# An expert layer's rows fetched by indirect DMA through a slot-to-token table, in place of one-hot products

## The chip, the core and the metric

The kernel runs on one core of a Trainium2 chip. The metric is the device time of one execution in microseconds (us), median over several runs. Engines are named as in the profile: PE (TensorE matmul), PEld (its weight loads), DVE (VectorE), ACT (ScalarE), POOL (GpSimd), SP (SyncE); SPq, ACTq and POOLq are the sequencers that issue their DMAs and branches.

## The reference

One layer over 512 tokens of width 1024. A token mixer (retention and mLSTM) makes up the first 1000 us and isn't touched but for its last rows. Then comes a mixture of 32 experts: each token picks one of four groups and two of its eight experts.

```
u2 = modulate(layer_norm(x), sh2, sc2)              # (512, 1024), float32
g  = top_1(softmax(u2 @ w_rg + b_rg))               # group
e1, e2 = top_2(softmax((u2 @ w_re + b_re)[g]))      # two experts of 8
y  = sum over the two: weight * ((silu(u2 @ w_e1[e]) * (u2 @ w_e3[e])) @ w_e2[e])
out = layer_norm(alpha * x + g2 * y) * ln2_g + ln2_b
```

Each expert has two matrices of 1024 x 512 and one of 512 x 1024 in float32, 2 MB each; all 32 together are 96 loads, 201 MB. The tokens of an expert are gathered into slots; 1024 assignments fall on 32 experts, unevenly.

## The kernel before

**Blocks.** An expert's tokens are worked on in blocks of 32 slots. The number of blocks is data: for experts 0 to 31 it is 1 1 1 1 1 1 1 1 1 2 2 1 1 2 1 1 2 2 1 1 2 1 1 1 5 3 2 1 3 2 1 1, 48 in all. The block count `nblk[e]` is loaded into a register of every engine one expert ahead; block 2 is inside `If(n >= 2)` (line 1576), block 3 inside `If(n > 2)` (line 1580), later ones inside further branches in `several` (lines 1493 to 1523).

**Loads.** `load(n)` (lines 925 to 941) issues the 96 weight loads on SP's queue (line 936), in order of expert. They go into a ring of 10 slots, RING = (2, 6, 2): two slots that are there early, six that come free after the mixer, two in the pool of the expert loop. Load n+10 is issued by SP after expert n/3 has used slot n. From load 10 on a load also waits until load n - 3 has landed (lines 937 to 939), so at most three are under way.

**Rows of an expert.** The normalised rows u2 are held in three bf16 parts whose sum is the float32 value: `u2[0..2]`, made per 128 tokens by `part_1` (line 1254: the first part by ScalarE, the remainder written back into `UP`) and `part_2` (line 1260). A one-hot matrix (`one_hot`, line 1169, VectorE: position of a token among its expert's slots equals slot number) times these parts gives the rows of the slots, transposed as the next product wants them. For experts 0 and 1 that is done ahead of the loop, 128 tokens at a time as they come ready: `gather_of` (line 1173, products at line 1177). For the others `gather(e, GN)` (line 1414, products at line 1424) does it inside the loop for a group of 64 slots of each of two (experts 2, 3) or four experts (4 to 7, 8 to 11, and so on), 96 products of up to 256 columns; it stands in experts 1, 3, 7, 11, 15, 19, 23 and 27, between that expert's hidden and output products. `slots_in` (line 1428, copies at 1432) copies the 64 slots of the next expert from PSUM.

**One block.** `hidden_q` (line 1459, 64 products at 1464, 32 slots wide) makes both hidden matrices in PSUM; `swiglu` (lines 1445 to 1447) combines them on ScalarE and VectorE; `turned` (line 1450) transposes the result twice on TensorE (line 1454) and copies it on ScalarE (line 1456); `output_q` (line 1469, 32 products at 1475) multiplies by the third matrix and VectorE scales the result (line 1477). Rows are stored to `y_d` in memory: the first two blocks from `yt` on ScalarE's queue (lines 1573 and 1579), the third and later ones from the two halves of `yq` by four DMAs on GpSimd's queue (line 1505).

**Third and later blocks.** `more(b, xT)` (line 1479) makes the rows of blocks 3 and 4 (then 5 and 6) at once by another one-hot (line 1482) and 96 products of 64 columns (line 1488), copied by ScalarE and VectorE (lines 1490, 1491).

**Order.** TensorE's order in the loop is as written (`manual_schedule(engines={EN.PE})`, lines 1557 to 1583), and so is SP's; the other engines' instructions are placed by the framework's scheduler. In one expert TensorE does:

```
t0 = hidden_q(xT, w, 0, gated("t0"))
if e + 1 in groups: xg = gather(start, GN)
output_q(t0, w[2], yt[:, 0:256])
with tc.If(n >= 2):
    output_q(hidden_q(xT, w, 1, gated("t1")), w[2], yt[:, 256:512])
    with tc.If(n > 2):
        several(e, w, n, xT, yq)
```

Behind expert 31 an indirect DMA on GpSimd (line 1605, 8 of them) fetches the two result rows of each token from `y_d` through `yrow`, and the weighted sum and last norm follow.

## Time and profile before

| | |
|---|---|
| median of 3 runs | 1661.74 us (1660.68 to 1661.85) |
| profiled execution, its own time | 1671.75 us |
| its span in the trace | 1669.7 us |
| mean granted TensorE clock | 0.922 |
| busy: PE, PEld | 1402.2 us (84%), 1101.1 us (66%) |
| busy: DVE, ACT, POOL | 783.6, 426.4, 185.1 us |
| HBM read, written | 307.37 MB, 33.57 MB |
| token mixer and routing | up to 1000.8 us |
| experts 0 to 3 | 1000.8 to 1058.6 us |
| experts 4 to 23 | 1058.6 to 1413.6 us |
| experts 24 to 31 | 1413.6 to 1629 us |
| sum and last norm | 1629 to 1669.7 us |

The boundaries of the experts are the starts of their first hidden products (line 1464). The profiled execution is one run with the hardware profiler on; all times of rows are its own. A granted clock of 1 is 2.4 GHz on TensorE, half of it the lower level; between them lies the mean of a stretch that has both. The DMA share is the mean busy share of 16 DMA engines.

### The profile page before, as it was taken

How to read it: one execution, taken by the hardware profiler on the slowest of the kernel's cores; microseconds unless marked ns; L12 is line 12 of the kernel's file. 1: busy time of each engine (PE TensorE's matmuls, PEld its weight loads, DVE VectorE, ACT ScalarE, POOL GpSimd, SP SyncE). 2: the span in 40 equal slices, each digit the busy share in tenths (PEclk: the TensorE clock that was granted, in tenths of full speed). 3: DMA queues.
4: the chain of work that ended last, by engine and by line, in shares of the span. 5: the costliest groups of instructions: out<-in, count | busy, mean ns of one | idle time of the engine just before them, and what ended most of it. 6: DMA issues, size and time to landing. Idle time of an engine off the chain costs nothing. (4 is left out here: it accounts for less than half of the span.)

```text
span 1669.7 us, 28900 instructions
## 1 busy us (share of the span) xinstructions
PE 1402.2 (84%) x11759; PEld 1101.1 (66%) x11759; DVE 783.6 (47%) x1893; ACT 426.4 (26%) x768; POOL 185.1 (11%) x113
## 2 busy tenths in 40 slices
PE   5999988999999999999999956666657677777774
PEld 3887977989798988989887744443434344445431
DVE  7757277485656565574777882211111111111115
ACT  3422244353444444443432220000000000000001
POOL 0101055143100000000023340000000000100003
PEclk9999999999999999999999968997889889888787
DMA  9414964244412131121656668989999989348444
GB/s 351 126 64 142 291 222 150 88 155 122 113 52 70 58 95 58 57 70 65 210 190 202 262 253 334 363 321 366 376 383 381 362 356 419 126 165 318 183 171 154
DMA packets 155844, 344.12 MB, mean 206 GB/s; under 512 B 18152, under 2 KB 110712, under 8 KB 147396
## 3 DMA queue, kind: packets, MB, share of 16 engines
q1 hardware_dynamic: 147544, 328.38, 54.7%
q10 hardware_dynamic: 6252, 7.73, 1.3%
q0 software_dynamic: 1792, 4.85, 0.8%
q8 instruction: 129, 2.11, 0.5%
q14 instruction: 127, 1.04, 0.2%
HBM read 307.37 MB, written 33.57 MB: 204 GB/s over the span
## 5 line engine op out<-in xcount | busy, mean ns | idle before, releaser
L1464 PE MATMUL ps_h<-w,xT 128*32 128x256 f32 x3072 | 220.2, 438 | 92.5 <-DVE xT L1432 34.4
L1464 PEld LDWEIGHTS ps_h<-w,xT 128*32 128x32 f32 x3072 | 121.4, 126 | 193.4 <-issue 132.2
L187 DVE TENSOR_TENSOR w_lo<-raw,w_hi 128x1024 fp32r<-128x1024 f32 x96 | 128.9, 1366 | 25.6 <-ACT w_hi L186 25.5
L1446 DVE SCALAR_TENSOR_TENSOR t<-t,ps_h 64x256 f32<-64x256 f32 x48 | 19.8, 412 | 256.8 <-ACT t L1445 256.8
L1475 PE MATMUL ps_y<-w,hT 128*32 128x256 f32 x1536 | 117.2, 457 | 19.8 <-ACT hT L1456 18.4
L1445 ACT ACTIVATE t<-ps_h 64x256 f32<-64x256 f32 x48 | 18.1, 377 | 427.9 <-PE ps_h L1464 386.1
L186 ACT ACTIVATE w_hi<-raw 128x1024 fp32r<-128x1024 f32 x96 | 96.1, 1050 | 58.8 <-PE ps_t L207 18.0
L550 POOL TENSOR_TENSOR macc<-macc,mw 128x1024 f32<-128x1024 f32 x32 | 82.2, 2570 | 101.2 <-ACT mw L549 51.5
L1475 PEld LDWEIGHTS ps_y<-w,hT 128*32 128x32 f32 x1536 | 52.0, 125 | 61.2 <-ACT hT L1456 25.4
L206 PE MATMUL ps_q<-u_lat,w_hi 128*128 128x512 f32 x192 | 78.8, 410 | 2.4 <-ACT u_lat L312 1.7
L1424 PE MATMUL xg<-sg,u 128*128 128x256 bf16 (+1 forms) x768 | 80.1, 266 | 0.0
L1477 DVE TENSOR_TENSOR yt<-ps_y,g2q 128x256 f32<-128x256 f32 x43 | 18.3, 425 | 129.4 <-PE ps_y L1475 119.4
L207 PE MATMUL ps_q<-u_lat,w_hi 128*128 128x512 f32 x192 | 77.9, 406 | 0.2 <-DVE u_lat L313 0.2
L208 PE MATMUL ps_q<-u_lat,w_lo 128*128 128x512 f32 x192 | 77.7, 405 | 0.0
L1424 PEld LDWEIGHTS <-u 128*128 128x128 bf16 x768 | 70.5, 98 | 10.7 <-issue 3.3
L1432 DVE COPY xT<-xg 128x128 f32<-128x128 f32 (+1 forms) x120 | 30.0, 295 | 96.9 <-PE xg L1424 62.6
L1505 POOL DMA_DIRECT2D y_d<-yq x20 | 10.2, 510 | 577.0 <-DVE yq L1477 455.6
L206 PE MATMUL ps_g<-w_hi,u_lat 128*128 128x256 f32 x256 | 72.6, 284 | 0.0
L208 PE MATMUL ps_g<-w_hi,u_lat 128*128 128x256 f32 x256 | 72.6, 283 | 0.0
L207 PE MATMUL ps_g<-w_lo,u_lat 128*128 128x256 f32 x256 | 72.5, 283 | 0.0
L207 PE MATMUL ps_v<-w_lo,u_lat 128*128 128x256 f32 x256 | 72.3, 282 | 0.0
L206 PE MATMUL ps_v<-w_hi,u_lat 128*128 128x256 f32 x256 | 72.3, 282 | 0.0
(394 smaller groups left out, 3450.7 us busy)
## 6 DMA issues: line engine op xcount, KB each, us to landing
w<-in_w_e_dram SPq DMA_DIRECT2D x96, 2048.0 KB
raw<-in_w_in_dram SPq DMA_DIRECT2D x40, 1024.0 KB
mw<-in_w_ada_dram SPq DMA_DIRECT2D x32, 512.0 KB
y_d<-plain SPq DMA_DIRECT2D x28, 512.0 KB
wada<-in_w_ada_dram SPq DMA_DIRECT2D x4, 2048.0 KB
y_d<-yt ACTq DMA_DIRECT2D x43, 128.0 KB
tanh_d<-tg SPq DMA_DIRECT2D x16, 256.0 KB
br_d<-rt SPq DMA_DIRECT2D x16, 256.0 KB
```

The costliest lines, as they stand in the source:

```text
L186: S.activation(h_, r_, AF.Copy)
L187: V.tensor_sub(l_, r_, f32(h_))
L206: PE.matmul(ps, lh, rh, start=first, stop=False)
L207: PE.matmul(ps, lh, rl, start=False, stop=False)
L208: PE.matmul(ps, ll, rh, start=False, stop=last)
L550: G.tensor_add(acc, acc, w)
L1424: PE.matmul(xg[j // step][:, j % step], u2[s_][:, i, j * P:(j + 1) * P], sg[:, i], start=(i == 0 and s_ == 0), stop=(i == 3 and s_ == 2))
L1432: V.tensor_copy(xT[:, j:j + step, :], xg[j // step][:, :, n, :])
L1446: V.scalar_tensor_tensor(t, t, 1.0, ps[0:64, 0:256], op0=OP.add, op1=OP.mult)
L1464: PE.matmul(ps[32 * a:32 * a + 32, 0:256], x[:, kt, 32 * b:32 * b + 32], w[a // 2][:, kt, 256 * (a % 2):256 * (a % 2) + 256], start=(kt == ...
L1475: PE.matmul(py[32 * a:32 * a + 32, 0:256], hT[:, kt % 2, 32 * (kt // 2):32 * (kt // 2) + 32], w2[:, kt, 256 * a:256 * a + 256], start=(kt ...
L1477: V.tensor_mul(yq, py[:, 0:256], g2q)
```

## The change

Rows of slots are no longer made by one-hot products inside the loop. `part_1` also stores the float32 rows to `u_d` in memory on ScalarE's queue (each token's 1024 values as four rows of 256), and writes the remainder into `xrs` in place of `UP`; `keep(3)`, which stores `xrs[3]`, comes earlier. After the routing, VectorE works out for each assignment the place of its slot; eight indirect DMAs on GpSimd scatter the token numbers into a table `inv_d` in memory (zeroed at the start), four DMAs load it back as `inv`, one copy per quarter of the partitions, and VectorE adds the quarter's number. `fetch(at, ...)` is an indirect DMA on GpSimd: it takes 128 rows of 1 KB from `u_d`, that is 32 slots x four quarters, to 128 partitions. `facing` turns them with two transposes on TensorE and one VectorE copy into the form that `hidden_q` wants.

Experts 0 to 3 are still made by one-hot products, now all four ahead of the loop (`gather_of` 256 columns wide, in four banks). For expert e >= 4 the first 32 rows are fetched into `xr` (two buffers): those of experts 4 and 5 ahead of the loop, those of e + 3 in expert e behind the facing of e + 1, which stands between the hidden and the output product of e. The second 32 rows are fetched inside `If(n >= 2)` into `xr1` (one buffer) and turned there. Third and later blocks copy their column of the table to `ix` on GpSimd, fetch into `xr2`, and turn; their stores are on GpSimd's queue as before. `yq` holds one block in place of two. The three parts of u2 live in a pool that is closed before the loop; the ring gets an eleventh slot in the loop's pool.

```diff
-RING = (2, 6, 2)
+RING = (2, 6, 3)
+NC = 112
...
+    u_d = dram.tile([4 * T, 256], F32, name="u_d")
+    inv_d = dram.tile([32 * NC, 1], I32, name="inv_d")
...
+        SP.dma_start(inv_d.rearrange("(s c) o -> s (c o)", c=NC), plain[0:32, 0:NC].bitcast(I32))
...
-    u2p = root.enter_context(tc.tile_pool(name="u2p", bufs=1))
-    u2 = [u2p.tile([P, 4, D], BF, name=f"u2{s}") for s in range(3)]
...
+    u2 = [bc.tile([P, 4, D], BF, name=f"u2{s}") for s in range(3)]
...
+    own = moec.tile([P, 5], F32, name="own")
+    SP.dma_start(own, I["small"][:, 640:645])
+    owni = moec.tile([P, 5], I32, name="owni")
+    V.tensor_copy(owni, own)
...
-                PE.matmul(xg[j // 4][:, j % 4], u2[s_][:, i, j * P:(j + 1) * P], sg,
-                          start=(i == 0 and s_ == 0 and j % 4 == 0), stop=(i == 3 and s_ == 2 and j % 4 == 3))
+                PE.matmul(xg[j // 2][:, j % 2], u2[s_][:, i, j * P:(j + 1) * P], sg,
+                          start=(i == 0 and s_ == 0 and j % 2 == 0), stop=(i == 3 and s_ == 2 and j % 2 == 1))
...
-        eng.tensor_sub(UP[i][:, c], UP[i][:, c], u2[0][:, i, c])
+        S.dma_start(u_d[4 * P * i:4 * P * i + 4 * P, :].rearrange("(p a) f -> p (a f)", a=4)[:, c], UP[i][:, c])
+        eng.tensor_sub(xrs[i][:, c], UP[i][:, c], u2[0][:, i, c])
 
     def part_2(i, eng, js=slice(0, NK)):
         c = slice(js.start * P, js.stop * P)
-        S.activation(u2[1][:, i, c], UP[i][:, c], AF.Copy)
-        eng.tensor_sub(u2[2][:, i, c], UP[i][:, c], u2[1][:, i, c])
+        S.activation(u2[1][:, i, c], xrs[i][:, c], AF.Copy)
+        eng.tensor_sub(u2[2][:, i, c], xrs[i][:, c], u2[1][:, i, c])
...
-        xg = xg_banks(2, 2)
+        xg = [gps.tile([P, 2, 4, 64], F32, tag=f"g{a}", name="xg") for a in range(4)]
         for b in range(2):
-            one_hot(sg0[:, b], b, 0, 2)
+            one_hot(sg0[:, b], b, 0, 4)
...
+        keep(3)
...
-    def gather(e, GN):
-
-        sg = m1p.tile([P, 4, 4, 64], BF, tag="sg", name="sg")[:, :, 0:GN]
-        for i in range(4):
-            one_hot(sg[:, i], i, e, GN)
-        xg = xg_banks(GN, 4 if GN == 4 else 2)
-        step = NK // len(xg)
-        for j in range(NK):
-            for i in range(4):
-                for s_ in range(3):
-                    PE.matmul(xg[j // step][:, j % step], u2[s_][:, i, j * P:(j + 1) * P], sg[:, i],
-                              start=(i == 0 and s_ == 0), stop=(i == 3 and s_ == 2))
-        return xg
...
+    def slots_of(b):
+        return mb.tile([P, 2, 4, 32], F32, tag=f"xT{b}", name="xT", bufs=1 if b else 2)
+
+    def slots_in(n, b):
+
+        xT = slots_of(b)
+        for a in range(4):
+            V.tensor_copy(xT[:, :, a, :], xg[a][:, :, n, 32 * b:32 * b + 32])
+        return xT
+
+    def fetch(at, tag, bufs):
+
+        xr = mr.tile([P, 256], F32, tag=tag, name="xr", bufs=bufs)
+        G.indirect_dma_start(out=xr, out_offset=None, in_=u_d, in_offset=bass.IndirectOffsetOnAxis(ap=at, axis=0),
+                             bounds_check=4 * T - 1, oob_is_err=False)
+        return xr
+
+    def facing(xr, b, pool, tag):
+
+        pt = pool.tile([P, 512], F32, tag=tag, name="ps_x")[:, 0:256].rearrange("p (c q) -> p c q", c=2)
+        for c in range(2):
+            PE.transpose(pt[:, c, :], xr[:, c * P:(c + 1) * P], ident)
+        xT = slots_of(b)
+        V.tensor_copy(xT.rearrange("p c a s -> p c (a s)"), pt)
...
-    def more(b, xT):
-
-        sb = m1p.tile([P, 4, 64], BF, tag="sb", name="osb")
-        V.tensor_tensor(sb, iota[:, 0:64].rearrange("p (o s) -> p o s", o=1).to_broadcast([P, 4, 64]),
-                        rme[:, :, b:b + 1].to_broadcast([P, 4, 64]), op=OP.is_equal)
-        ps = hps.tile([P, 512], F32, tag="ph", name="ps_or").rearrange("p (j s) -> p j s", j=NK)
-        for j in range(NK):
-            for i in range(4):
-                for s_ in range(3):
-                    PE.matmul(ps[:, j], u2[s_][:, i, j * P:(j + 1) * P], sb[:, i],
-                              start=(i == 0 and s_ == 0), stop=(i == 3 and s_ == 2))
-        S.copy(xT[:, 0:4], ps[:, 0:4])
-        V.tensor_copy(xT[:, 4:8], ps[:, 4:8])
-
-    def several(e, w, n, xT, yq):
-
-        for b in range(2):
-            V.tensor_scalar(rme[:, :, b:b + 1], rm[:, :, e:e + 1], -64.0 * (b + 1), None, op0=OP.add)
-
-        base = nc.values_load(orow[0:1, e:e + 1], min_val=64 * NE, max_val=64 * NE + 1024)
-
-        def some(b, row):
-
-            y = yq[:, b, :]
-            output_q(hidden_q(xT, w, b), w[2], y)
+    def several(e, w, n, yq):
+
+        base = nc.values_load(ocol[0:1, e:e + 1], min_val=2 * NE, max_val=2 * NE + 32)
+
+        def some(col):
+
+            ix = mr.tile([P, 1], I32, tag="ix", name="ix", bufs=2)
+            G.tensor_copy(ix, inv[:, bass.ds(col, 1)])
+            x = facing(fetch(ix, "xr2", 2), 2, tps, "tp")
+            output_q(hidden_q(x, w, gated("t")), w[2], yq)
             for a in range(4):
-                stored(G.dma_start(y_d[bass.ds(row, 32), 256 * a:256 * a + 256], y[32 * a:32 * a + 32, :]))
+                stored(G.dma_start(y_d[bass.ds(col * 32, 32), 256 * a:256 * a + 256], yq[32 * a:32 * a + 32, :]))
 
         tc.mark_branch_hint_location(f"more{e}d", smin(n >> 2, 1), engines={EN.PE})
-        more(0, xT)
-        some(0, base)
+        some(base)
         with tc.If(n > 3, label=f"more{e}d"):
-            some(1, base + 32)
+            some(base + 1)
             with tc.If(n > 4):
-                more(1, xT)
-                some(0, base + 64)
+                some(base + 2)
                 with tc.If(n > 5):
-                    some(1, base + 96)
+                    some(base + 3)
                     with tc.If(n > 6):
-                        V.tensor_scalar(rme, rme, -64.0, None, op0=OP.add)
-                        with tc.For_i(6, n, 2) as i:
-                            V.tensor_scalar(rme, rme, -64.0, None, op0=OP.add)
-                            more(0, xT)
-                            for b in range(2):
-                                some(b, base + i * 32 - 64 + 32 * b)
+                        with tc.For_i(6, n) as i:
...
+        rb8 = m1p.tile([P, 8], I32, name="rb8")
+        V.tensor_copy(rb8, r8)
+        V.tensor_scalar(rb8, rb8, 5, None, op0=OP.logical_shift_right)
+        V.tensor_scalar(sel[:, 0, :], sel[:, 0, :], 1.0 / 32, None, op0=OP.mult)
+        V.scalar_tensor_tensor(sel[:, 0, :], r8, float(NC), sel[:, 0, :], op0=OP.mult, op1=OP.add)
+        pos = m1p.tile([P, 8], I32, name="pos")
+        V.scalar_tensor_tensor(pos, rb8, 1.0 - 32 * NC, sel[:, 0, :], op0=OP.mult, op1=OP.add)
+    tok = []
+    for n in range(8):
+        q_ = G.indirect_dma_start(out=inv_d, out_offset=bass.IndirectOffsetOnAxis(ap=pos[:, n:n + 1], axis=0),
+                                  in_=owni[:, n // 2:n // 2 + 1], in_offset=None, bounds_check=32 * NC - 1, oob_is_err=False)
+        for o in tok:
+            tc.declare_no_dep(q_.ins, o.ins, reason="each assignment has its own slot")
+        tok.append(q_)
+    inv = m1p.tile([P, NC], I32, name="inv")
+    for a in range(4):
+        G.dma_start(inv[32 * a:32 * a + 32, :], inv_d.rearrange("(s c) o -> s (c o)", c=NC))
+    V.tensor_tensor(inv, inv, owni[:, 4:5].to_broadcast([P, NC]), op=OP.add)
+    xr = {e: fetch(inv[:, 2 * e:2 * e + 1], "xr", 2) for e in (4, 5)}
...
+            yq = mr.tile([P, 256], F32, tag="yq", name="yq", bufs=1)
             xT = xnext
             tc.mark_branch_hint_location(f"more{e}a", smin(n >> 1, 1), engines={EN.PE})
-            t0 = hidden_q(xT, w, 0, gated("t0"))
-            if e + 1 in groups:
-                start = e + 1
-                GN = groups[start]
-                xg = gather(start, GN)
+            t0 = hidden_q(xT, w, gated("t0"))
+            if e + 1 < 4:
+                xnext = slots_in(e + 1, 0)
+            elif e + 1 < NE:
+                xnext = facing(xr.pop(e + 1), 0, *((tps, "tp") if e == 3 else (gps, f"g{e % 4}")))
+                if e + 3 < NE:
+                    xr[e + 3] = fetch(inv[:, 2 * e + 6:2 * e + 7], "xr", 2)
             output_q(t0, w[2], yt[:, 0:256])
             stored(S.dma_start(y_d[e * 64:e * 64 + 32, :].rearrange("s (a f) -> a s f", a=4), yt[:, 0:256]))
-            if e + 1 < NE:
-                xnext = slots_in(xg, e + 1 - start, GN)
             with tc.If(n >= 2, label=f"more{e}a"):
                 tc.mark_branch_hint_location(f"more{e}c", smin(n // 3, 1), engines={EN.PE})
-                output_q(hidden_q(xT, w, 1, gated("t1")), w[2], yt[:, 256:512])
+                x1 = slots_in(e, 1) if e < 4 else facing(fetch(inv[:, 2 * e + 1:2 * e + 2], "xr1", 1), 1, tps, "tp")
+                output_q(hidden_q(x1, w, gated("t1")), w[2], yt[:, 256:512])
                 stored(S.dma_start(y_d[e * 64 + 32:e * 64 + 64, :].rearrange("s (a f) -> a s f", a=4), yt[:, 256:512]))
                 with tc.If(n > 2, label=f"more{e}c"):
-                    several(e, w, n, xT, yq)
+                    several(e, w, n, yq)
             for m in range(3):
                 load(3 * e + m + sum(RING))
```

## Rows read from the trace of the kernel before

**Rows 1.** The head of the page.

```profile
span 1669.7 us, 28900 instructions
```

**Rows 2.** Busy time by stretch; columns: stretch, length, five engines, clock, DMA share, GB/s.

```profile
core 0: us, PE busy (x) PEld busy (x) DVE busy (x) ACT busy (x) POOL busy (x), PEclk, DMA share, GB/s
997.00:1001.00 4.00, 2.88 (x28) 2.65 (x31) 3.12 (x24) 0.49 (x4) 0.00 (x0) 0.59 0.60 184
1058.00:1413.00 355.00, 244.17 (x3028) 146.46 (x3028) 58.55 (x178) 17.01 (x52) 0.00 (x0) 0.88 0.95 369
1413.00:1629.00 216.00, 160.71 (x2252) 95.05 (x2252) 34.21 (x104) 13.26 (x40) 10.19 (x20) 0.85 0.51 198
```

**Rows 3.** Waits of SP's queue, 1039 to 1302 us; columns: us, waits, us to landing.

```profile
SPq L936 <- DMA w<-in_w_e_dram: 231.8, 45, 7.9
```

**Rows 4.** The load line's issues, 1039 to 1302 us; least/mean/most ns, first and last.

```profile
L936 SPq DMA_DIRECT2D w<-in_w_e_dram x45: 327/331/379, 1039.2 to 1301.9; - x45
```

**Rows 5.** The load line's issues, 1394 to 1396 us.

```profile
L936 SPq DMA_DIRECT2D w<-in_w_e_dram x1: 332/332/332, 1395.5 to 1395.5; - x1
```

**Rows 6.** Busy time of line 1424 alone; columns: stretch, length, PE, PEld, clock, share, GB/s.

```profile
1058.00:1413.00 355.00, 53.27 (x480) 46.57 (x480) 0.88 0.95 369
```

**Rows 7.** Timeline of expert 24: start, length, engine, line; in brackets its wait.

```profile
1413.58 3.97 PE L1464 MATMUL ps_h<-w,xT 128*32 128x256 f32 x64 [1.25 <-DMA w<-in_w_e_dram]
...
1419.78 2.54 PE L1475 MATMUL ps_y<-w,hT 128*32 128x256 f32 x32 [0.43 <-ACT hT L1456]
...
1422.07 4.78 PE L1464 MATMUL ps_h<-w,xT 128*32 128x256 f32 x64
...
1429.01 1.93 PE L1475 MATMUL ps_y<-w,hT 128*32 128x256 f32 x32 [0.36 <-ACT hT L1456]
...
1435.45 3.66 PE L1464 MATMUL ps_h<-w,xT 128*32 128x256 f32 x64 [0.46 <-ACT xT L1490]
...
1441.27 3.53 PE L1475 MATMUL ps_y<-w,hT 128*32 128x256 f32 x32 [0.37 <-ACT hT L1456]
...
1444.55 3.79 PE L1464 MATMUL ps_h<-w,xT 128*32 128x256 f32 x64
1444.84 0.42 DVE L1477 TENSOR_TENSOR yq<-ps_y,g2q 128x256 f32<-128x256 f32 x1 [4.39 <-PE ps_y L1475]
1445.59 2.30 POOL L1505 DMA_DIRECT2D y_d<-yq  x4 [449.66 <-DVE yq L1477]
```

**Rows 8.** Timeline ahead of expert 0: the last early products.

```profile
998.12 2.72 PE L1177 MATMUL xg<-sg,u 128*128 128x128 bf16 x24 [1.22 <-DVE sg L1170]
```

**Rows 9.** Groups by line, 900 to 1670 us: busy, mean ns, idle before.

```profile
L1605 POOL DMA_INDIRECT ys<-y_d,yrow x8 | 8.0, 1002 | 53.2 <-PE ps_z L1613 51.0 <-issue 2.1
...
L1206 PE MATMUL ps_t<-small,xr 128*128 128x128 f32 x32 | 5.8, 338 | 5.2 <-DVE xr L1196 5.2
```

**Rows 10.** The DMA view: a queue (packets, MB, share); issues (count, KB, us to landing).

```profile
q10 hardware_dynamic: 6252, 7.73, 1.3%
...
y_d<-yt ACTq DMA_DIRECT2D x43, 128.0 KB
...
y_d<-yq POOLq DMA_DIRECT2D x20, 32.0 KB, 3.0
...
ys<-y_d,yrow POOLq DMA_INDIRECT x8, 5.7
```

**Rows 11.** Timeline of ScalarE and its queue, 1145 to 1162 us.

```profile
1145.20 1.05 ACTq L1573 DMA_DIRECT2D y_d<-yt  x1
...
1160.78 1.03 ACTq L1579 DMA_DIRECT2D y_d<-yt  x1
1162.02 0.38 ACT L1445 ACTIVATE t<-ps_h 64x256 f32<-64x256 f32 x1 [11.77 <-DMA y_d<-yt]
```

**Rows 12.** Busy time of line 1488 alone, in two stretches; columns as Rows 6.

```profile
1453.00:1460.00 7.00, 5.03 (x96) 4.99 (x96) 0.61 0.09 21
1490.00:1495.00 5.00, 2.96 (x96) 2.84 (x95) 1.00 0.01 3
```

**Rows 13.** ScalarE's branch and its store, 1187 to 1200 us.

```profile
L1576 ACTq COMPARE_BRANCH  x1: 45/45/45, 1192.1 to 1192.1; - x1
...
L1573 ACTq DMA_DIRECT2D y_d<-yt x1: 1052/1052/1052, 1195.3 to 1195.3; - x1
```

More of the change, by code (lines that the diff above doesn't have):

```diff
@@ L974, in build @@
     Eb = bc.tile([P, 4, NE], BF, name="Eb")
-    rm = moec.tile([P, 4, NE], F32, name="rm")
+    rm = bc.tile([P, 4, NE], F32, name="rm")
     wk = moec.tile([P, 4, 2], F32, name="wk")
@@ L980, in build @@
     obase = moec.tile([P, NE], F32, name="obase")
-    orow = moec.tile([P, NE], I32, name="orow")
+    ocol = moec.tile([P, NE], I32, name="ocol")
     eoff = moec.tile([P, NE], F32, name="eoff")
     SP.dma_start(eoff, I["small"][:, 320:352])
+    own = moec.tile([P, 5], F32, name="own")
+    SP.dma_start(own, I["small"][:, 640:645])
+    owni = moec.tile([P, 5], I32, name="owni")
+    V.tensor_copy(owni, own)
     def permuted(name, src):
@@ L1162, in affine_a @@
         eng.tensor_add(dst, dst, bias)
-    def xg_banks(GN, n):
-        ts = [gps.tile([P, NK // n, GN, 64], F32, tag=f"g{a}", name="xg") for a in range(n)]
-        return ts
     def one_hot(sg, i, e, GN):
@@ L1267, in build @@
     lt3 = p2.tile([P, 1, 36], F32, tag="lt1", name="lt1")
-    sg0 = bc.tile([P, 4, 2, 64], BF, name="sg0")
+    sg0 = bc.tile([P, 4, 4, 64], BF, name="sg0")
     with tc.manual_schedule(engines={EN.PE, EN.DVE, EN.Activation, EN.Pool}):
@@ L1410, in build @@
     g2q = m1p.tile([P, 256], F32, name="g2q")
-    rme = m1p.tile([P, 4, 2], F32, name="rme")
     scat = []
-    def gather(e, GN):
-        sg = m1p.tile([P, 4, 4, 64], BF, tag="sg", name="sg")[:, :, 0:GN]
-        for i in range(4):
-            one_hot(sg[:, i], i, e, GN)
-        xg = xg_banks(GN, 4 if GN == 4 else 2)
-        step = NK // len(xg)
-        for j in range(NK):
-            for i in range(4):
-                for s_ in range(3):
-                    PE.matmul(xg[j // step][:, j % step], u2[s_][:, i, j * P:(j + 1) * P], sg[:, i],
-                              start=(i == 0 and s_ == 0), stop=(i == 3 and s_ == 2))
-        return xg
-    def slots_in(xg, n, GN):
-        xT = mb.tile([P, NK, 64], F32, tag="xT", name="xT")
-        step = 4 if GN == 2 else 2
-        for j in range(0, NK, step):
-            V.tensor_copy(xT[:, j:j + step, :], xg[j // step][:, :, n, :])
+    def slots_of(b):
[16 more added lines that the diff above has]
+        V.tensor_copy(xT.rearrange("p c a s -> p c (a s)"), pt)
         return xT
@@ L1530, in build @@
         SP.dma_start(g2q[32 * b:32 * b + 32, :], mod_d[3, 256 * b:256 * b + 256].rearrange("(o d) -> o d", o=1).to_broadcast([32, 256]))
-    groups = {0: 2, 2: 2, **{e: 4 for e in range(4, NE, 4)}}
-    start, GN = 0, 2
     nb = nc.values_load(nblk[0:1, 0:1], min_val=0, max_val=16)
     with tc.manual_schedule(engines={EN.DVE}):
-        xnext = slots_in(xg, 0, 2)
+        xnext = slots_in(0, 0)
         ov = m1p.tile([P, NE], F32, tag="ov", name="ov")
```

18 lines of the change are left out of this document (9 added, 9 removed).

## The prediction

> **What bounds the kernel now.** I read the span first [rows 1], then the busy time of the stretches of the expert loop [rows 2]. From 1058 to 1413 us (experts 4 to 23) TensorE has work for 244 of 355 us and the DMA share is 0.95; from 1413 to 1629 (experts 24 to 31) TensorE is busy for 161 of 216 us and the share falls to 0.51. The second stretch is a chain of TensorE, ScalarE and VectorE, since the weights lie ready. For the first, the waits of the load queue are to be seen: between 1039 and 1302 us it waited for its own earlier loads in 45 of its waits, 232 of 263 us [rows 3]. Those 45 loads stand 262.7/44 = 5.97 us apart [rows 4], 17.9 us for an expert's three. So in that stretch the transfers and the chain are nearly tied: 20 experts need 358 us of loads, and the chain took 355.
>
> How much could the first stretch give if TensorE cost nothing? A load is issued only when the one three before it has landed. Load 76 (counted from 0, by the order of issue) goes out at 1395.5 us [rows 5], so load 73, the second matrix of expert 24, was there by then. Expert 24 began at 1413.6 us [rows 7]. The floor is thus 18 us earlier, no more.
>
> **What goes.** Five gathers of one-hot products lie in the first stretch, 53.3 us together, 10.7 each [rows 6]. Without one, the hidden product's end and the output product stand 1441.27 - 1439.11 = 2.2 us apart [rows 7]; a gather fills these, so each gives 8.5 us: 42.5 in the first stretch, 8.5 at expert 3, 8.5 at expert 27. The three to five `more` products of the second stretch lie between an output product's end at 1430.94 and the next hidden product at 1435.45, 4.5 us [rows 7].
>
> **What comes, ahead of the loop.** The early products now take 256 columns. The last 24 stand ahead of expert 0 and took 2.72 us for 128 columns [rows 8], at a granted clock of 0.59 from 997 to 1001 us [rows 2]: twice that at most, +2.7; I take 2.4, and +1.0 for wider one-hots and for the copy to memory of the last rows, which must land before their tile is overwritten (0 to 3). Five more DMA issues on ScalarE's queue and the eight scatters, four table loads and two fetches on GpSimd's cost nothing: ScalarE is idle most of that time, GpSimd had nothing to do until 1445.59 [rows 7], and expert 4's rows are wanted only some 40 us later. If that cover went (VectorE's one addition to the table ahead of expert 1's work), expert 1 would slip by some 10 us, under the loads. With the gather at expert 3 gone, expert 4 starts 3.4 - 8.5 = -5.1 us.
>
> **The eleventh slot** I cost at nothing: the loads are paced by one another [rows 3], and in the second stretch they are early. It would be worth one load, 6 us, where loads decide; against that, the slot of load 9 now lies on memory that the last early product still reads, so that load starts some 6 us later.
>
> **The first 32 rows of experts 4 to 31** are fetched two experts ahead, about 35 us (355/20 x 2). Their two transposes of 0.34 us [rows 9] fall into the 2.2 us between hidden and output product: nothing. Their traffic counts only at the floor: a packet of the store queue took 1.3% of 16 x 1669.7 us over 6252 packets = 56 ns [rows 10], so 128 packets on 16 engines 0.44 us; 28 fetches up to expert 24 make 12 us. Floor: 1395.5 - 2 + 12 = 1405, 8.6 earlier than now.
>
> **The second 32 rows** are the term that decides. Eleven experts need them (43 stores of `yt`, 32 of them first blocks): six in the first stretch, and 24, 25, 26, 28, 29. Today the second hidden product starts at 1422.07, as the first output product ends [rows 7], 4.5 us after the first hidden product's end at 1417.55. Now a fetch must come first, and GpSimd issues it behind the fetch for expert e+3, whose tile is free only after this expert's transposes. Count from the hidden product's end: transposes 0.75, issue of the earlier fetch 1.0 [rows 9] with two short waits 0.3, landing L, two transposes 0.7, a VectorE copy with its waits 0.7: 3.45 + L against 4.5. The delay is L - 1.05.
>
> L is not in this trace. From below: 3.0 us, the 32 KB stores that GpSimd issues into quiet queues (the last gather's 5.7 us is for eight of 512 KB) [rows 10]. From above: a 128 KB store in the same 1 KB packets, issued at 1145.20 between loads, let go of the next store and of ScalarE's queue only at 1160.8 [rows 11]: 15.5 us. I take the middle, 9.3: the fetch is issued some 8 us after the previous expert's end has set off three loads of 6 us each, so about half of these are still ahead of it. Delay 8.2 us each; 3 for expert 29, when one load is left.
>
> **The third and later blocks.** Block 3 is fetched right behind block 2: 4.5 us become 1.4, -3.1. Block 4 (expert 24) follows today at 1444.55 without a gap [rows 7]. Its fetch will stand behind the stores of block 3 in GpSimd's queue: VectorE's 0.42 at 1444.84, the stores from 1445.59 for 2.30 [rows 7], index copy and branch 0.5, landing 4.0 (quiet by then; 3.0 to 15.5), transposes and copy 1.4, minus what runs beside: +9.0. Block 5 pays the same less its old products (5.03 us [rows 12] and 1.4 around them): +2.6.
>
> **The clock.** An order product took 2.96 us where the clock was 1.00 and 5.03 at 0.61 [rows 12]. A hidden product behind a wait of 8 us starts at the low level. It takes 3.66 us at the high one [rows 7], 7.3 at worst; I take +1.2 for each of 13 blocks that wait (0 to 3.7).
>
> **Sum.** First stretch: -5.1 + 6 x 8.2 - 42.5 + 6 x 1.2 = +8.8, so expert 24 starts at 1422, past the floor of 1405: the chain decides. Second stretch: expert 24 8.2 - 3.1 + 9.0 + 2.6 = 16.7; 25 5.1; 26 8.2; 27 -8.5; 28 5.1; 29 3; clock 7 x 1.2 = 8.4: +38. Behind expert 31 nothing changes. Together +46.8 on the profiled execution's 1671.75 us, which is itself 10 us above the median of 1661.74; carried to the median, 1708.
>
> **Rivals.** *The fetch lands as in quiet queues* (L 3.5). For: GpSimd's own stores do [rows 10]. Against: the share of 0.95 [rows 2] and [rows 11]. Delays of 2.5 each; the first stretch then ends at the floor, -8.6; the second is 11 - 0.6 + 2.5 - 8.5 - 0.6 + 2.5 + 3 = +9: 1662, no change. By the Trainium skill ("DMA: Bandwidth & Descriptors", section "Anatomy of one DMA") a DMA from GpSimd costs 2.0 us and its bytes at 436 GB/s, an estimate of 2.3 us for 128 KB. The 15.5 us of [rows 11] speak against it in the first stretch; by it the sum would be some 1657.
>
> *The fetch of the second rows is issued early* (faster). If GpSimd's queue has the branch of expert e ahead of the fetch for e+3, it is a whole expert early, and a second block costs 1.4 us. First stretch at the floor, -8.6; second stretch 9.9 - 1.7 + 1.4 - 8.5 - 1.7 + 1.4 + 2 = +3: 1656. For it: ScalarE's store at 1195.3 stands behind the branch at 1192.1 though the program has it ahead [rows 13], so such an order occurs. Against: that store's input came late, while the fetch waits only for transposes ahead of the output product. It decides from the point where the fetch is issued over 10 us ahead of need.
>
> *The clock and the load queue cost more.* With every delayed block at the low level throughout, 3.7 + 1.9 us for 13 blocks, 73 in place of 16: 1765; with L at 15.5 and the clock as taken, 1771. For: both levels are in [rows 12]. Against: the mean stays at 0.85 in a stretch that waits a good deal already [rows 2]. The Trainium skill ("TensorE: Matmul & The Clock Gate", section "Part 1: The HAM clock gate") says that low is the resting state, and that only activity lifts it; a change that takes dense products away and adds waits would lose by it. The rows agree on the two levels.
>
> *The change does not do what it says*: the extra slot runs no load earlier because loads wait for loads. That is my forecast for it already.
>
> **Chances.** Forecast 0.42 (its own range 1680 to 1740), quiet fetch 0.22, early fetch 0.20, dearer 0.16. Some 0.2% is what a measurement of this kernel can tell from no change: 1658.4 to 1665.1. Of the quiet case 0.06 falls below, 0.10 inside; of the early one 0.17 below, 0.03 inside. Faster 0.23, same 0.13, slower 0.64. The range reaches to 1652, short of the early case's best, and up to 1760, into the dearer one.
>
> **What would show it.** Right: the DMA issues of `xr` from GpSimd, those of second blocks with 8 us and more to landing; TensorE's transposes of these rows waiting some 8 us for a DMA in eleven experts; expert 24 starting near 1422; block 4 waiting about 9 us for a fetch issued behind four stores. Wrong: a landing of 3 to 5 us between loads, or second fetches issued before their expert begins, with expert 24 at about 1405 and load waits ending the idle time of hidden products.

## The result: 1744.6 us after 1661.2, and where the 83 us lie

The changed kernel took 1744.64 us (median of 4 runs, 1742.04 to 1747.41), the kernel before 1661.21: a ratio of 1.0507, interval 1.0484 to 1.0530. The profiled executions differ by 1742.04 - 1671.75 = 70.3 us, their spans by 1740.4 - 1669.7 = 70.7; the rest is that the one shown of before lies 10 us above its median and the one of after 2.6 below. The head of the page after:

```profile
span 1740.4 us, 26902 instructions
```

Its busy time by stretch (experts 0 to 3, 4 to 23, 24 to 31; columns as in [rows 2]):

```profile
1001.30:1069.30 68.00, 30.06 (x395) 15.57 (x395) 11.46 (x48) 2.62 (x8) 13.21 (x15) 0.75 0.78 304
1069.30:1441.90 372.60, 215.77 (x2602) 108.22 (x2604) 41.95 (x104) 17.03 (x52) 26.00 (x26) 0.82 0.89 358
1441.90:1697.30 255.40, 152.82 (x1806) 74.91 (x1806) 30.41 (x78) 11.79 (x36) 26.90 (x40) 0.79 0.46 180
```

TensorE has 28 us less to do in experts 4 to 23 than in [rows 2] (215.8 for 244.2), and yet they take 372.6 us for 355: the DMA share fell from 0.95 to 0.89 and the granted clock from 0.88 to 0.82. Neither engine nor loads bound it; it waits. The stages, from the starts and ends of hidden and output products in both timelines:

| stage | before | after | forecast | measured |
|---|---|---|---|---|
| up to expert 0 | 1000.8 | 1001.3 | +3.4 | +0.5 |
| experts 0 to 3 | 57.8 | 68.0 | -8.5 | +10.2 |
| experts 4 to 23 | 355.0 | 372.6 | +13.9 | +17.6 |
| experts 24 to 31 | 215.1 | 255.4 | +38.0 | +40.3 |
| behind | 41.0 | 43.1 | 0 | +2.1 |
| sum | 1669.7 | 1740.4 | +46.8 | +70.7 |

**Expert 1 waits for the table.** The timeline between expert 0 and 1:

```profile
1016.88 0.97 POOL L1552 DMA_INDIRECT inv_d<-owni,pos  x1 [0.30 <-issue]
1023.45 2.05 POOL L1559 DMA_DIRECT2D inv<-inv_d  x4 [5.60 <-DMA inv_d<-owni,pos]
1033.41 0.28 DVE L1560 CUSTOM_DVE_ANT_0 inv<-owni,inv 128x224 uint16<-128x224 uint16 x1 [16.84 <-DMA inv<-inv_d]
1035.27 5.08 PE L1473 MATMUL ps_h<-w,xT 128*32 128x256 f32 x64 [24.43 <-DVEq L1581]
1035.36 0.62 DVE L1426 COPY xT<-xg 128x64 f32<-128x64 f32 x4 [1.68 <-DVEq L1581]
```

The last scatter is issued at 1016.9, the table's loads from 1023.4, and VectorE sits in front of its one addition for 16.8 us. Everything that VectorE and TensorE do for expert 1 is queued behind it: a gap of 24.4 us in place of 2.2.

**A second block waits for its rows.** Expert 9 in the timeline:

```profile
1155.20 0.44 PE L1440 MATMUL ps_x<-small,xr 128*128 128x128 f32 x2
1155.91 1.00 POOL L1432 DMA_INDIRECT xr<-u_d,inv  x1 [16.23 <-PE ps_x L1440]
1157.21 1.00 POOL L1432 DMA_INDIRECT xr<-u_d,inv  x1 [0.30 <-issue]
1157.77 3.54 PE L1484 MATMUL ps_y<-w,hT 128*32 128x256 f32 x32 [0.43 <-ACT hT L1465]
...
1165.66 0.66 PE L1440 MATMUL ps_x<-small,xr 128*128 128x128 f32 x2 [4.35 <-DMA xr<-u_d,inv]
...
1166.84 5.84 PE L1473 MATMUL ps_h<-w,xT 128*32 128x256 f32 x64 [0.52 <-DVE xT L1442]
```

The second fetch goes out 1.3 us behind the one for expert 12 and its rows are turned 8.4 us later. The second hidden product starts 11.6 us after the first ends (1155.20 to 1166.84); in [rows 7] it was 4.5. Over the six such experts of the stretch what follows the first output product grew from 50.0 to 98.0 us. The clock costs too: this product takes 5.84 us at a granted clock of 0.50 in its first us and 0.62 over its length; the same product took 3.66 us at 1.00 before.

**Later blocks and expert 29.** Expert 24's fourth block and the second block of 29, in the timeline:

```profile
1485.91 2.33 POOL L1499 DMA_DIRECT2D y_d<-yq  x4 [29.44 <-DVE yq L1486]
...
1488.75 1.09 POOL L1432 DMA_INDIRECT xr<-u_d,ix  x1 [0.32 <-POOL ix L1495]
1491.68 0.66 PE L1440 MATMUL ps_x<-small,xr 128*128 128x128 f32 x2 [6.54 <-DMA xr<-u_d,ix]
...
1647.13 0.44 PE L1440 MATMUL ps_x<-small,xr 128*128 128x128 f32 x2
...
1654.69 1.08 POOL L1432 DMA_INDIRECT xr<-u_d,inv  x1 [9.53 <-issue]
1659.67 0.66 PE L1440 MATMUL ps_x<-small,xr 128*128 128x128 f32 x2 [8.05 <-DMA xr<-u_d,inv]
```

Block 4's fetch stands behind the four stores of block 3 and then lands in 2.9 us, with no load under way. At expert 29 GpSimd comes 7 us late to its fetch. What held it is in its queue at line 1503, the end of the branch of expert 28 (waits, and their first and last start):

```profile
L1503 POOLq EVENT_SEMAPHORE  x5: 17/43/43, 1645.1 to 1651.1; - x5
...
L1503 POOLq INC_SWDGE_SEM  x1: 1657/1657/1657, 1651.2 to 1651.2; - x1
```

It leaves that branch only when its own four stores, issued from 1642.8, have landed, the last at 1650.9.

### The profile page after: what moved, and what is told of

It is laid out like the page before. It is cut to its first block, busy times and chain, and to the rows that moved or that the text cites. A ratio compares the mean times of both kernels' runs of the same rounds, so it can differ in the third digit from the quotient of the medians.

```text
span 1740.4 us, 26902 instructions
## 1 busy us (share of the span) xinstructions
PE 1353.7 (78%) x10695; PEld 1027.2 (59%) x10695; DVE 759.3 (44%) x1794; ACT 425.9 (24%) x764; POOL 237.0 (14%) x174
## 5 line engine op out<-in xcount | busy, mean ns | idle before, releaser
L1473 PE MATMUL ps_h<-w,xT 128*32 128x256 f32 x3072 | 235.2, 466 | 133.4 <-PEq L1567 66.5
L1454 ACT ACTIVATE t<-ps_h 64x256 f32<-64x256 f32 x48 | 18.1, 377 | 587.0 <-PE ps_h L1473 587.0
L1442 DVE COPY xT<-ps_x 128x256 f32<-128x256 f32 x44 | 18.7, 425 | 302.4 <-PE ps_x L1440 302.2
L1484 PE MATMUL ps_y<-w,hT 128*32 128x256 f32 x1536 | 124.8, 481 | 20.4 <-ACT hT L1465 17.5
L1432 POOL DMA_INDIRECT xr<-u_d,inv x39 | 39.4, 1010 | 458.9 <-PE ps_x L1440 420.5
L1440 PE MATMUL ps_x<-small,xr 128*128 128x128 f32 x88 | 22.5, 345 | 76.1 <-DMA xr<-u_d,inv 63.0
L906 POOL TENSOR_TENSOR raw<-raw,g 128x2048 f32<-128x2048 f32 x4 | 18.5, 4636 | 450.9 <-PE ps_b L214 417.1
L212 PE MATMUL ps_v<-w_hi,u_lat 128*128 128x256 f32 x256 | 72.2, 282 | 0.0
L214 PE MATMUL ps_v<-w_hi,u_lat 128*128 128x256 f32 x256 | 72.0, 281 | 0.0
```

What stands on the lines that cost most here:

```text
L212: PE.matmul(ps, lh, rh, start=first, stop=False)
L214: PE.matmul(ps, ll, rh, start=False, stop=last)
L906: G.tensor_mul(raw, raw, g1.rearrange("p (o f) -> p o f", o=1).to_broadcast([P, NK, 256]))
L1432: G.indirect_dma_start(out=xr, out_offset=None, in_=u_d, in_offset=bass.IndirectOffsetOnAxis(ap=at, axis=0), bounds_check=4 * T - 1, oob_i ...
L1440: PE.transpose(pt[:, c, :], xr[:, c * P:(c + 1) * P], ident)
L1442: V.tensor_copy(xT.rearrange("p c a s -> p c (a s)"), pt)
```

## The experiments

Every kernel is the changed one with the edit shown. The ratios are to the kernel before on the same chip; its median was 1657.5 to 1664.6 us there, so that medians of different rows are compared by their ratios where a few us matter. Stage lengths are worked out as in the table above; whole spans of single profiles are compared with care, since expert 0 started anywhere from 997.6 to 1007.1 us in kernels that don't differ ahead of it.

| kernel | median, us | ratio to before |
|---|---|---|
| changed kernel | 1744.64 | 1.0507 (1.0484 to 1.0530) |
| table_add_on_gpsimd | 1733.89 | 1.0453 (1.0404 to 1.0502) |
| second_rows_early | 1691.16 | 1.0211 (1.0159 to 1.0264) |
| two_loads_under_way | 1744.58 | 1.0505 (1.0444 to 1.0566) |
| one_load_under_way | 1866.81 | 1.1250 (1.1190 to 1.1309) |
| ten_slots | 1744.08 | 1.0468 (1.0404 to 1.0531) |
| later_stores_on_scalar | 1729.65 | 1.0399 (1.0342 to 1.0456) |
| second_rows_first | 1744.79 | 1.0483 (1.0425 to 1.0541) |
| second_rows_first_in_order | 1748.30 | 1.0501 (1.0461 to 1.0542) |
| early_rows_and_table | 1726.32 | 1.0376 (1.0333 to 1.0420) |
| rows_early_stores_on_gpsimd | 1661.17 | 1.0007 (0.9983 to 1.0032) |
| rows_early_gpsimd_in_order | 1686.94 | 1.0152 (1.0122 to 1.0182) |
| rows_early_add_on_vector | 1675.09 | 1.0080 (1.0052 to 1.0109) |

### The table's addition

```diff
-    V.tensor_tensor(inv, inv, owni[:, 4:5].to_broadcast([P, NC]), op=OP.add)
+    G.tensor_tensor(inv, inv, owni[:, 4:5].to_broadcast([P, NC]), op=OP.add)
```

> Only the addition to the table is moved from VectorE to GpSimd. Theory (the addition held VectorE, and with it the copies for expert 1, until the table had landed, and nothing covers that): the 24.4 us ahead of expert 1 become 2 to 4, expert 4 starts near 1048 instead of 1069.3, expert 24 near 1421 instead of 1442, and the median is about 1724. Rival (the wait was covered by the weight loads): the gap closes, but hidden products of experts 5 to 12 then wait for weights, expert 24 still starts near 1442, and the median stays within 5 us of 1744.

The gap fell to 7.3 us, but experts 0 to 3 take 59.2 us and not 47, and the median gained half of what was expected. The timeline shows the next in line:

```profile
1015.01 4.93 PE L1473 MATMUL ps_h<-w,xT 128*32 128x256 f32 x64 [7.29 <-DVEq L1581]
...
1030.67 0.37 POOL L1560 TENSOR_TENSOR inv<-inv,owni 128x112 int32<-128x112 int32 x1 [8.39 <-DMA inv<-inv_d]
...
1039.09 1.10 POOL L1432 DMA_INDIRECT xr<-u_d,inv  x1 [8.05 <-DMA y_d<-yt]
...
1047.54 0.41 PE L1440 MATMUL ps_x<-small,xr 128*128 128x128 f32 x2 [4.25 <-DMA xr<-u_d,inv]
```

Expert 4's rows are fetched 8 us after the addition, behind a branch in GpSimd's queue, and land 8.4 us later; expert 3's transposes wait for them. So the wait was on the path, as the theory says, and the rival falls: experts 5 to 12 don't wait for weights. But the table itself is late, and only part of the gap is to be had.

### How long a fetch takes to land

```diff
-            tc.add_manual_dep(loads[n].ins, loads[n - 3].ins.name,
+            tc.add_manual_dep(loads[n].ins, loads[n - 2].ins.name,
```

and the same with n - 1.

> A weight load waits for the one two before it instead of three. Theory (landing is long because of the loads that lie ahead in the DMA engines): second rows land about 6 to 7 us after their issue instead of 8.5, loads keep a pace of 6 to 6.5 us and stay ahead of the products, and the median is 15 to 28 us lower, near 1722. Rival (landing is set by GpSimd's queue and by the fetch ahead of it): landing stays at 8 to 9 us and the median within 5 us of 1744.

> A weight load waits for the one just before it. Theory: second rows land in about 5 us, as the one of expert 29 did with one load under way; the loads themselves now stand about 8 us apart, 24 us for an expert where the products take 18.6, so that experts 5 to 24 wait for weights and the median is some 1800. Rival (landing is set by GpSimd's queue): landing stays at 8 to 9 us. What tells them apart is the time from issue to transposes, not the median.

From the issue of the second rows to their transposes, in experts 9, 10, 13, 16, 17 and 20: 8.4, 9.3, 8.8, 8.2, 7.9, 8.1 us in the changed kernel (mean 8.4); 7.3, 8.1, 8.5, 7.6, 7.9, 7.8 with two loads (7.9); 5.4, 3.9, 3.3, 3.7, 3.0, 3.6 with one (3.8). Expert 10 in the timeline of the kernel with two loads:

```profile
1179.84 1.00 POOL L1432 DMA_INDIRECT xr<-u_d,inv  x1 [0.30 <-POOLq L1586]
...
1187.96 0.66 PE L1440 MATMUL ps_x<-small,xr 128*128 128x128 f32 x2 [5.64 <-DMA xr<-u_d,inv]
```

The same in the timeline of the kernel with one:

```profile
1217.26 1.00 POOL L1432 DMA_INDIRECT xr<-u_d,inv  x1 [0.30 <-issue]
...
1221.14 0.41 PE L1440 MATMUL ps_x<-small,xr 128*128 128x128 f32 x2 [1.41 <-DMA xr<-u_d,inv]
```

The busy time over experts 4 to 23, with two loads and with one (columns as in [rows 2]):

```profile
1070.70:1453.30 382.60, 228.54 (x2600) 112.33 (x2601) 41.95 (x104) 17.05 (x52) 25.98 (x26) 0.79 0.90 345
1073.30:1563.20 489.90, 237.97 (x2602) 112.33 (x2603) 41.94 (x104) 17.05 (x52) 26.00 (x26) 0.73 0.70 257
```

The same two fetches in the same order take some 8 us or, in five of six, under 4, so it isn't GpSimd's queue: that rival falls. In experts 9, 13, 16 and 20 of the kernel with one load the transposes waited for no DMA, so that their times are upper bounds. But the number of loads ahead isn't the measure either, as the first expectation had it: with two under way the DMA engines are as full (share 0.90 in this stretch), and landing and median stay; with one the share is 0.70, and the fetch lands in half the time, though a load was under way at each of the six. That it is the share that decides fits the three kernels and isn't shown beyond them. The price is the weights: 489.9 us for 60 loads, 8.2 each, and a median of 1867 where some 1800 was expected.

### Second rows fetched one expert early

```diff
+    xr1 = {}
...
                 if e + 3 < NE:
                     xr[e + 3] = fetch(inv[:, 2 * e + 6:2 * e + 7], "xr", 2)
+                xr1[e + 1] = fetch(inv[:, 2 * e + 3:2 * e + 4], "xr1", 2)
...
-                x1 = slots_in(e, 1) if e < 4 else facing(fetch(inv[:, 2 * e + 1:2 * e + 2], "xr1", 1), 1, tps, "tp")
+                x1 = slots_in(e, 1) if e < 4 else facing(xr1.pop(e), 1, tps, "tp")
...
+            xr1.pop(e, None)
```

> The second 32 rows of expert e + 1 are fetched in expert e, for every expert from 4 on whether it has a second block or not, into two buffers. Theory (the second block waits for a fetch that is issued just before it and lands 8.5 us later under weight loads): the transposes of second rows follow the first output product without a DMA wait, what follows the first output product in an expert of two blocks falls from about 16.5 us to 8 or 9, expert 24 starts at 1400 to 1412 (then the load pace of about 6 us each decides, slack 0 to 5 us), the last stretch is some 45 us shorter, and the median is about 1665 (1655 to 1685). Rival (GpSimd's queue, which takes its fetches one behind another, is the limit): 28 more fetches make first rows late too, and the median is 1744 or more.

The wait is gone in every expert: what follows the first output product fell from about 16.5 to about 10 us (98.0 to 60.6 over six), experts 4 to 23 from 372.6 to 346.4. The median gained 53 us (49 by the ratios) of the 80 expected. Part of the rest lies in the first hidden products of experts 4 to 23, which took 122.0 us for 108.2 in the changed kernel; what made them longer isn't shown. Expert 24 now waits for its weights, in the timeline:

```profile
1411.12 0.63 PE L1473 MATMUL ps_h<-w,xT 128*32 128x256 f32 x4 [2.74 <-DMA w<-in_w_e_dram]
...
1417.10 4.97 PE L1473 MATMUL ps_h<-w,xT 128*32 128x256 f32 x60 [5.35 <-DMA w<-in_w_e_dram]
```

These waits come to 8.1 us, no more than the gaps of 4.8 and 3.5 us ahead of and inside the same product in the changed kernel. But since expert 24 is early, the fetch of its fourth block, still behind the stores, meets loads under way: 10.2 us to land instead of 2.9.

### The eleventh slot

```diff
-RING = (2, 6, 3)
+RING = (2, 6, 2)
```

> RING is (2, 6, 2) again. Theory (in the changed kernel weights lie ready 16 us and more before their hidden product, so a slot more or less moves no product): the smallest margin falls by some 6 us to about 10, the median stays within 5 us of 1744. Rival (the extra slot is what kept experts 5 to 24 fed): hidden products wait for weights and the median rises by 10 us or more.

As the theory had it: 1744.08 for 1744.64. The smallest margin is expert 9's: by the records of the loads' semaphores its first matrix landed 17.5 us ahead of the hidden product's start in the changed kernel and 5.9 here, its second 11.4 ahead (not 16 and more, as the expectation has it) and here 0.4 behind. The gap inside that product is 2.1 us here and 2.2 there, so the matrix that came late cost nothing that can be seen. The slot is worth nothing while rows are what is late.

### The order of the two fetches

```diff
-                if e + 3 < NE:
-                    xr[e + 3] = fetch(inv[:, 2 * e + 6:2 * e + 7], "xr", 2)
...
+            if 4 <= e + 1 and e + 3 < NE:
+                xr[e + 3] = fetch(inv[:, 2 * e + 6:2 * e + 7], "xr", 2)
             for m in range(3):
```

> The fetch of the first rows for expert e + 3 is moved behind the branch of expert e, so that the fetch of the second rows is the first that GpSimd issues after the transposes. Theory (the loads in the DMA engines make the landing long): counted from the first hidden product's end the second transposes come at 8.5 to 9.5 us instead of 10.4, counted from the issue still 8 us or so; median some 10 to 15 us lower, about 1731. Rival (the fetch ahead of it in the same queue makes it long): the landing from issue falls to about 5 us and the median to about 1700.

It told nothing apart: the scheduler put that fetch at the head of the next expert, ahead of its branch, so the second rows were still issued second (1.3 us behind, landing 8.8 us later in expert 10). The same edit with GpSimd in the order of the program (`EN.Pool` in both `manual_schedule` sets; for that, the stores of later blocks lose their freedom from one another):

> The changed kernel with the fetch for expert e + 3 behind the branch of expert e and GpSimd in the order of the program, so that the second rows are fetched first. Theory (loads in the DMA engines make the landing long): from the first hidden product's end to the second transposes 8.5 to 9.5 us instead of 10.4, from the issue some 8 us as before; median some 10 to 15 us below 1744. Rival (the fetch ahead of it makes the landing long): some 5 us from the issue, median about 1700.

Neither came about. With the fetch for e + 3 out of the way, GpSimd runs ahead through the branch of the next expert, and in experts 9 to 24 the second rows are fetched 6.8 to 15.3 us before the first hidden product ends. Experts 4 to 23 take 347.1 us: this is the rival of the early fetch, which the prediction priced. What it gave was lost behind expert 24, where every store of a later block now waits for the one before it to land, and fetches stand behind them, as GpSimd's timeline shows:

```profile
1514.34 0.50 POOL L1500 DMA_DIRECT2D y_d<-yq  x1 [1.94 <-DMA y_d<-yq]
1519.71 0.50 POOL L1500 DMA_DIRECT2D y_d<-yq  x1 [4.87 <-DMA y_d<-yq]
...
1526.30 0.50 POOL L1500 DMA_DIRECT2D y_d<-yq  x1 [6.09 <-DMA y_d<-yq]
1535.09 1.07 POOL L1432 DMA_INDIRECT xr<-u_d,inv  x1 [8.29 <-issue]
```

That part is the edit's own doing, and the landing in the other order stays untried.

### Stores of later blocks

```diff
-                stored(G.dma_start(y_d[bass.ds(col * 32, 32), 256 * a:256 * a + 256], yq[32 * a:32 * a + 32, :]))
+                stored(S.dma_start(y_d[bass.ds(col * 32, 32), 256 * a:256 * a + 256], yq[32 * a:32 * a + 32, :]))
```

> Only the four stores of third and later blocks move from GpSimd's queue to ScalarE's. Theory (the fetches of blocks 4 and 5 stand behind those stores): TensorE's two waits of 6.5 us in expert 24 go, the work behind its first output product falls from 60.9 to 45 to 49 us; at expert 29 GpSimd no longer waits for its own stores before it passes a branch, 21.2 becomes about 17; together 16 to 22 us, median about 1725. Rival (the wait moves to ScalarE, whose queue now holds the stores ahead of the next activation): half of that or less.

The median came out near the theory's, by two errors that cancel. Behind the first output products of 24 and 29 it is 43.3 and 9.7 us for 60.9 and 21.2, more than expected. But between hidden and output products of experts 4 to 23 26 us were added, also in experts without a third block. The same edit with the two others above (early second rows, addition on GpSimd):

> Three edits together: the table's addition on GpSimd, second rows fetched one expert early, and the four stores of third and later blocks on ScalarE's queue. Theory (each wait has its own cause): expert 4 starts some 9 us earlier than with early second rows alone, expert 24 at 1395 to 1405, where the load pace decides; the work behind expert 24's first output product falls from 64.6 us to 42 to 48, since blocks 4 and 5 no longer fetch behind stores; median 1645 to 1670, no more than a tie with the kernel before, as the loads' pace of some 6.3 us with the fetches between them takes back what the gathers gave. Rival (the waits only move): the median stays above 1680.

Worse by 35 us (27 by the ratios) than early second rows alone. ScalarE in expert 7 of that kernel, whose hidden product ended at 1117.1, in the timeline:

```profile
1129.24 1.05 ACTq L1582 DMA_DIRECT2D y_d<-yt  x1
1131.61 0.38 ACT L1454 ACTIVATE t<-ps_h 64x256 f32<-64x256 f32 x1 [22.44 <-ACTq L1583]
```

The activation stands behind the store of the expert before, and that is held until 1129.2. The store waits for a semaphore that weight loads use too, and the records tell who lets it go: SP's queue waits at the end of its branch for the loads under way (its waits end at 1118.6, 1124.0 and 1128.9), renews the semaphore at 1129.16, and the store goes at 1129.24. All nine stores of ScalarE that stood at such a semaphore for 8 us and more between 1066 and 1471 us went 0.08 or 0.09 us behind a renewal by SP. The waits of ScalarE name SP's queue as well (us, times, longest):

```profile
ACT t L1454 <- SPq L1588: 67.4, 4, 21.1
```

In [rows 11] the store was held at a shared semaphore too, but there it was a weight load's landing at 1160.70 that let it go.

### All rows early, stores left on GpSimd

```diff
+        near = [rows_of(base + b) for b in range(3)]
-        some(base)
+        some(base, near[0])
         with tc.If(n > 3, label=f"more{e}d"):
-            some(base + 1)
+            some(base + 1, near[1])
...
```

where `rows_of` is the copy and the fetch that stood in `some`; with early second rows and the addition on GpSimd.

> The table's addition on GpSimd, second rows one expert early, and the rows of blocks 3 to 5 fetched together ahead of block 3; the stores of later blocks stay on GpSimd's queue. Theory (in early_rows_and_table the stores moved to ScalarE were what cost, and each removed wait is worth its own length where the loads allow it): no output product waits more than 5 us for ScalarE, the work behind expert 24's first output product is 42 to 47 us instead of 64.6, expert 24 starts at 1395 to 1408, median 1650 to 1675. Rival (the waits only move): above 1680.

As the theory had it: level with the kernel before (1.0007, 0.9983 to 1.0032). No version was faster than the kernel before. Expert 24's transposes of blocks 2 to 5, in the timeline, wait for nothing, and the stores no longer stand before a fetch:

```profile
1431.27 0.56 PE L1440 MATMUL ps_x<-small,xr 128*128 128x128 f32 x2
...
1441.74 0.45 PE L1440 MATMUL ps_x<-small,xr 128*128 128x128 f32 x2
...
1452.08 0.44 PE L1440 MATMUL ps_x<-small,xr 128*128 128x128 f32 x2
1452.91 2.33 POOL L1502 DMA_DIRECT2D y_d<-yq  x4 [21.39 <-DVE yq L1486]
...
1462.41 0.44 PE L1440 MATMUL ps_x<-small,xr 128*128 128x128 f32 x2
```

Behind its first output product 39.9 us are left (46.6 before the change, 60.9 after); experts 24 to 31 take 199.7 us, 15 less than before, experts 4 to 23 349.3. Two more tell what is left:

> As rows_early_stores_on_gpsimd, but GpSimd's instructions from the table's loads on stand in the order of the program, so that the fetches for experts 4 and 5 follow the table's addition at once and not behind the branches of the first experts. Theory: expert 3's transposes no longer wait for rows of expert 4 (its hidden and output product stand 2.5 us apart instead of 6.9), expert 4 starts some 5 us earlier, the median is 0 to 8 us below that of rows_early_stores_on_gpsimd, because the load pace takes part of it back. Rival (the program's order puts new waits into GpSimd's queue): equal or slower.

The fetch for expert 4 still came behind a branch (1044.5 us, the addition at 1035.9), expert 3 still waited, and the stores waited one for another as above: slower, as the rival had it.

> As rows_early_stores_on_gpsimd, but the table's addition is on VectorE again, so that expert 1 waits for the table. Theory (the loads take back what the chain gains ahead of expert 24): the gap of 24 us is back and expert 4 starts some 9 us later, counted from expert 0's start, but expert 24 only 0 to 6 us later, with weights landing no more than 5 us ahead of it or later than it wants them; the work behind expert 24's first output product stays at 40 to 47 us; median 1661 to 1670. Rival (the chain decides up to expert 24): the full 9 to 11 us remain, median 1670 to 1673.

1675.09: more than either expected. Counted from expert 0, expert 4 is 11.1 us later and expert 24 still 8.0. Now the weights decide there: the first matrix of 24 lands as its hidden product starts, the second 5.9 us later. Both answers hold at once: while expert 1 waits it also keeps its slots, so that the loads behind it start later, the first of expert 5 by 12.3 us and the first of expert 24 by 14.2.

## Why the prediction was right, and the term that was not

**Forecast 1708, +47; measured 1744.6, +83; inside the range.** The mechanism of the likeliest case is the one that happened. Its time is not: 1744.6 lies 4.6 us above the 1680 to 1740 that this case was given for itself, in a part of the range that stood there for the dearer rival. That rival's conditions didn't come (L was 8.4 and not 15.5, and no block was at the low level throughout), so it is luck that the range reached so far. Step by step:

- *The gathers.* Time between hidden and output products of experts 4 to 23 fell by 43.8 us (93.6 to 49.8); 42.5 were forecast from [rows 6, 7].
- *Second rows.* L was taken as 9.3, between 3.0 and 15.5; it measured 8.4 in the first stretch. The issue was put 2.05 us behind the hidden product's end and came 1.9 behind it. From the end of the first hidden product to the start of the second it was 4.4 us before and 11.6 after (means of six): a delay of 7.2, with 8.2 forecast. That loads make it long was shown by the kernel with one load; that it is the term that decides, by early second rows, -53 us. That 9.3 came so near is in part luck, since the upper bound of 15.5 was misread: the store at 1160.78 waited for a semaphore that it shares with a weight load issued at 1142.68, and that load's landing let it go. The last landing on record for the store of 1145.20 itself is at 1163.3, 18.1 us after its issue.
- *The quiet fetch.* Its price of 3.5 is right where it is quiet: 2.9 us in expert 24. The Trainium skill ("DMA: Bandwidth & Descriptors", section "Anatomy of one DMA") gives an estimate of 2.3 us for 128 KB; the quiet fetch of the trace is 0.6 us above it, and under loads, for which that section's formula has no term, the 8.4 us are 3.7 times as long.
- *Later blocks.* Expert 24 was forecast at +16.7 and, with the clock's 1.2 for its blocks 2, 4 and 5, at +20.3; what follows its first output product grew by 14.3. Experts 25 and 28 were forecast at +6.3 with the clock, and grew by 7.4 each. In expert 24 the four stores ahead of the fetch are the cause; with the rows fetched ahead of them it is gone.
- *The clock.* Six blocks at +1.2 made 7.2 us in the first stretch. These six hidden products took 33.2 us for 23.4, +9.8, each with a granted clock of 0.50 in its first us: the mechanism is right and its price too low. The first output products of the stretch took 7.1 us longer too, which no step had; the first hidden products 0.2. The granted clock is 0.82 for 0.88.
- *The slot.* Nothing, as costed.

**The step that failed** is in "What comes, ahead of the loop": "cost nothing", with the slip named as "some 10 us, under the loads" if VectorE's addition came ahead of expert 1's work. It came ahead, slipped 22.2 us and not 10, and nothing covered it: both matrices of expert 4's hidden product had landed 33 us before it started. The table's own chain was never added up, though [rows 9, 10] gave its outline; it measured eight scatters at 1.3 us, 6.5 for the last to land, four loads at 0.5, 8 to land. The scheduler's freedom to put the addition there was seen and given no chance of its own. With it the stage comes to +10.2 in place of -8.5, 19 of the 24 us that the sum missed.

**Smaller misses.** Expert 29 was costed at 3 and 1.2 for the clock and cost 13.4: that GpSimd must see its stores landed before it leaves a branch was not thought of. The second stretch came out near its forecast (+40.3 for +38.0) because this miss of 9.2 and the 6.0 that expert 24 was costed too high took most of each other back; that is luck. And 6.0 us came from gaps ahead of hidden products, which no step had. Two rows of TensorE's waits in experts 4 to 23 of the kernel before (us, times, longest):

```profile
PE ps_h L1464 <- DVE xT L1432: 25.5, 6, 5.9
PE ps_h L1464 <- PEq L1562: 21.7, 8, 4.7
```

The same view after, its first row:

```profile
PE ps_h L1473 <- PEq L1567: 63.0, 17, 6.2
```

After, TensorE's own sequencer ends 17 waits of up to 6.2 us, at the start of an expert, mostly where the one before had no second block and the body of its branch was jumped over. The Trainium skill ("Runtime: NRT & Kernel Launch", section "Instruction fetch mechanics") says that a taken branch to a page not yet loaded stalls until that page is fetched; the rows fit, and no run here tries it. Ahead of experts 8, 12, 16, 20 and 24 the gaps were 11.6 us together behind a gather and are 27.3 without one, so it may be that a gather of 8.5 us was also hiding part of such a stall. That is argued from these sums alone.

**Why there was little to win.** Even with all rows early experts 4 to 23 take 349 us, 6 less than before, and there the first matrix of expert 24 lands 5.8 us ahead of the hidden product's start, the second 0.6 behind it. The forecast's floor, less the fetches' own traffic, was the right frame, though its 18 us were 22: load 73 landed at 1391.4, and up to 1395.4 load 76 was held by a semaphore that a store shares. With all rows early loads 18 to 72 are issued 6.29 us apart, where [rows 4] has 5.97: 1.0 more for an expert's three, and two fetches at the forecast's 0.44 would make 0.9. That fits, but no run tries it. So the gathers lay where the loads decide nearly as much as TensorE, and where they did not, in experts 24 to 31, the gain is 15 us.

## What to carry to other kernels

A product that makes an operand costs its time on an engine, but it needs no notice; a fetch in its place costs the chain little if it is issued early (here 60.6 us behind six first output products for 50.0 before), and its whole landing if it is issued on demand, priced under the traffic that it will meet. Look at what is queued in front of it on the issuing engine (another fetch, stores, a branch) and behind the instruction that waits for its table. Before taking work off an engine, ask how soon the next limit comes: here the loads were some 20 us away.

## What was not expected of the hardware

The landing of 128 KB hardly depends on whether two or three loads are under way (7.9 and 8.4 us, share 0.90 and 0.89), and falls to 3.8 with one (share 0.70). In this program GpSimd waits for its stores to land before it passes the end of a branch that it entered: 5.6 us and 1.7 for the semaphores at expert 28. A store on ScalarE's queue was held by the weight loads on SP's, with which it shares a semaphore, and so kept back an activation that could have run 14.5 us earlier (1117.1 to 1131.6). A wait at expert 1 delayed not only the chain but the load stream, and 8 of 11 us were still there 20 experts later.
